# Both MLP products of a two-layer trunk in an order written by hand, with x fetched and turned beside the second product

## The chip, the cores and the metric

The kernel runs on one core of one Trainium2 chip. The metric is the device time of one execution in microseconds; less is better. A core has five engines that run their own instruction queues in order: TensorE (PE, the matmuls), VectorE (DVE), ScalarE (ACT), GpSimd (POOL) and SyncE (SP), which here issues nearly all DMA transfers. Engines meet through semaphores only. Data lives in SBUF (128 partitions), matmul results in PSUM (eight banks of 128 x 512 float32).

## The reference

The input is x, 1024 tokens x 1024 features, float32. Two layers follow, each a mixer and an MLP, and a last norm.

```python
for layer in range(DEPTH):
    h = rmsnorm(x, mix_norm_g[layer])
    x = x + (diff_attention(h, ...) if layer == 0 else recurrent_block(h, ...))
    x = x + sqrelu_mlp(rmsnorm(x, mlp_norm_g[layer]), mlp_w1[layer], mlp_w2[layer])
return rmsnorm(x, final_norm_g)

def sqrelu_mlp(h, w1, w2):          # w1: 1024 x 4096, w2: 4096 x 1024
    return jnp.square(jax.nn.relu(h @ w1)) @ w2
```

Only the two MLPs, `h @ w1` (the first product) and `relu(..)^2 @ w2` (the second), are touched by the change.

## The kernel before

**Numbers in two halves.** Each float32 operand is split into a high part (rounded by a ScalarE copy to fp32r) and a low part (operand minus high part, by VectorE; `split`, L83). A product then takes three matmuls: high x high, high x low, low x high.

**Seven products for eight.** Both MLP products are 2 x 2 block products computed with seven block products, by sums and differences of blocks (Winograd's form). The operands' sums are made on VectorE before they are split; the seven results are added up on the way out of PSUM. The norm's factor of a token is not applied to the first product's input: since relu squared is homogeneous, the second product's result is multiplied by `inv` = 1/(mean square + eps) (L895), spread over partitions for layer 0 (`spread`, L277), as a column per token block in layer 1.

**First product.** `parts_block` (L239) turns each block of x into the split block operands `self.sx[k]`, k = 0 to 3 (28 tiles of 128 x 1024), as the mixer's last product finishes, and stores x to DRAM (`xD`). The 32 blocks of 128 columns of `w1` are taken as 16 pairs, i and i+16. For each pair, `pair_weights` (L770) loads two blocks, makes the sums `s12` and `s34` and splits everything; `hidden_pair` (L794) does seven products of 12 matmuls (k = 0 to 3, three each; L809 to L811), adds them up in `ct` and `cl` (L814), applies relu and the square on ScalarE (L835, L836), makes the second product's sums (`h12`, `h34`, L840) and writes seven pieces of 128 x 512 to DRAM (`hid`, L843). In layer 1, pairs 3 to 10 each also turn one 128 x 1024 block of x (`turn_x`, L867): load from `xD`, eight transposes on TensorE (L874), a ScalarE copy (L876), a store to `xN`. After pair 1 the token's mean squares are summed on TensorE (L894).

**The planner.** Outside a `manual_schedule` block, the framework's planner orders the instructions of an engine by its own costs, and may put instructions of one pair ahead of another's. Inside such a block, the listed engines take the block's instructions in the order written; other instructions may still be put between them. Before, the first products are the planner's; the second products (L903) are in the written order on PE, ACT, DVE and SP.

**Second product.** `second` (L906) works through 56 slots of 24 matmuls (L1007 to L1009): 8 of kind P, 16 A, 16 B, 8 C and 8 D. P gives the first of the seven products, in banks `u` (two PSUM tiles of two banks each); A two at once, on `z` (four tiles of a bank) and further on `u`; B two, on `z` and `u`; C one on `z`; D one on `u`. A slot's operands are loaded four slots ahead (`load`, L931; at most four in the rings R and W) and made and split one slot ahead (`prepare`, L963). D of the last four slots is done one output block at a time. When a product is complete, `after` (L1069) empties its banks, and the rest of the adding goes into a list `side`, of which two or three steps run per slot (L1113). `x` itself is fetched in halves (`xr`, L1014) during B and added there. Where an output half is finished, `x_done` runs: in layer 0 the recurrence's norm and split (`norm_part`, L215), in layer 1 the final norm (`final_part`, L1135), which goes from ScalarE (squares) to VectorE to GpSimd (rsqrt) and back.

**Buffers.** Most tiles of 128 x 1024 float32 come from one ring, T, of 46; raw weights from R (4), some high parts and loaded hidden blocks from W (4).

Of the kernel before, what the change touches and what calls it, by code (L numbers as in the profile page):

```python
# [30 lines left out]
def rope_tables():  # L31

    inv = np.float32(1.0) / np.power(10000.0, np.arange(0, HD, 2) / HD).astype(np.float32)
    ang = np.arange(S, dtype=np.float32)[:, None] * inv[None, :]
    cos = np.cos(ang.astype(np.float64)).astype(np.float32).T
    sin = np.sin(ang.astype(np.float64)).astype(np.float32).T
    c = np.concatenate([cos, cos, cos, cos], axis=0)
    s = np.concatenate([-sin, sin, -sin, sin], axis=0)
    return np.ascontiguousarray(c), np.ascontiguousarray(s)


class Trunk:
# [727 lines left out]
    def pair_weights(self, w1, i):  # L770

        nc = self.nc
        top, low = (self.raw(w1[:, c : c + P].rearrange("(k p) m -> p k m", p=P), (P, NK, P)) for c in (i * P, DFF // 2 + i * P))
        a, b = slice(0, 4), slice(4, 8)
        s12, s34 = self.t4("s12", F32, (P, NK, P)), self.t4("s34", F32, (P, NK, P))
        sub = lambda out, x, y, op=ALU.subtract: nc.vector.tensor_tensor(out=out, in0=x, in1=y, op=op)  # L779
        sub(s12[:, a], low[:, a], low[:, b], ALU.add)  # L780
        sub(s12[:, b], s12[:, a], top[:, a])
        sub(s34[:, a], top[:, a], low[:, a])
        sub(s34[:, b], top[:, b], s12[:, b])
        th, tl = self.split(top, (P, NK, P), "wt", hi_tag="W")
        lw = self.t4("wl", F32R, (P, 2, 4, P))
        nc.scalar.activation(out=lw[:, 0], in_=low[:, b], func=AF.Copy)
        nc.vector.tensor_tensor(out=lw[:, 1], in0=low[:, b], in1=lw[:, 0].bitcast(F32), op=ALU.subtract)
        h12, l12 = self.split(s12, (P, NK, P), "ws", hi_tag="W")
        h34, l34 = self.split(s34, (P, NK, P), "ws")
        return {"A11": (th[:, a], tl[:, a]), "A12": (th[:, b], tl[:, b]), "A22": (lw[:, 0], lw[:, 1]),  # L790
                "S1": (h12[:, a], l12[:, a]), "S2": (h12[:, b], l12[:, b]),
                "S3": (h34[:, a], l34[:, a]), "S4": (h34[:, b], l34[:, b])}

    def hidden_pair(self, w, i, last):  # L794
# [6 lines left out]
        mm = nc.tensor.matmul  # L801
        p1, p2, p4 = self.acc1(), self.accg(), self.accg()
        p67, p53 = self.acc2(), self.acc2()
        l, r = slice(0, CH), slice(CH, S)

        def product(a, b, bank):
            for k in range(4):
                (ah, al), (bh, bl) = w[a], self.sx[k][b]
                mm(bank, ah[:, k], bh, start=k == 0, stop=False)  # L809
                mm(bank, ah[:, k], bl, start=False, stop=False)  # L810
                mm(bank, al[:, k], bh, start=False, stop=k == 3)  # L811

        def add(out, x, y, op=ALU.add):
            nc.vector.tensor_tensor(out=out, in0=x, in1=y, op=op)  # L814

        top, low = self.t4("ct"), self.t4("cl")
        product("A11", "B11", p1)
        nc.scalar.activation(out=top[:, l], in_=p1, func=AF.Copy)
        product("S2", "T2", p67[:, l])
        add(low[:, l], top[:, l], p67[:, l])  # L820
        product("S1", "T1", p53[:, l])
        add(low[:, r], low[:, l], p53[:, l])
        product("S4", "B22", p53[:, r])
        add(top[:, r], low[:, r], p53[:, r])
        product("S3", "T3", p67[:, r])
        both = low.rearrange("p (h c) -> p h c", c=CH)
        add(both, both, p67[:, None, r].to_broadcast([P, 2, CH]))
        product("A12", "B21", p2)
        add(top[:, l], top[:, l], p2)
        product("A22", "T4", p4)  # L830
        add(low[:, l], low[:, l], p4, ALU.subtract)


        for c in (top, low):
            nc.scalar.activation(out=c, in_=c, func=AF.Relu)  # L835
            nc.scalar.activation(out=c, in_=c, func=AF.Square)  # L836
        a12, a34 = self.t4("h12", F32, (P, 2, CH)), self.t4("h34", F32, (P, 2, CH))
# [4 lines left out]
        f = self.hid[i]  # L842
        put = lambda at, src: nc.sync.dma_start(out=f[:, at], in_=src)  # L843
        put(0, top[:, l])
        put(5, low[:, l])
        if last:
            two(a12[:, 0], top[:, r], low[:, r], ALU.add)
            two(a12[:, 1], a12[:, 0], top[:, l])
            two(a34[:, 0], top[:, l], top[:, r])
            two(a34[:, 1], low[:, l], a12[:, 1])  # L850
            put(3, a34[:, 1])
            put(6, low[:, r])
        else:
            two(a12[:, 0], top[:, r], top[:, l])
            two(a12[:, 1], low[:, r], a12[:, 0])
            two(a34[:, 0], low[:, r], top[:, r])
            two(a34[:, 1], low[:, l], a12[:, 1])
            put(3, low[:, r])
            put(6, a34[:, 1])
        put(slice(1, 3), a12)  # L860
        put(4, a34[:, 0])

    def mlp_first(self, layer):

        self.w = self.pair_weights(self.ins["mlp_w1"][layer], 0)

    def turn_x(self, m):  # L867

        nc = self.nc
        t = self.t4("xm")  # L870
        nc.sync.dma_start(out=t, in_=self.xD[m])
        ps = self.acc2()
        for k in range(NT):
            nc.tensor.transpose(ps[:, k * P : (k + 1) * P], t[:, k * P : (k + 1) * P], self.ident)  # L874
        kept = self.t4("xk", F32, (P, NT, P))
        nc.scalar.activation(out=kept, in_=ps.rearrange("p (k c) -> p k c", c=P), func=AF.Copy)  # L876
        nc.sync.dma_start(out=self.xN.rearrange("(t p) c -> p t c", p=P)[:, :, m * P : (m + 1) * P], in_=kept)

    def mlp(self, layer, last):

        nc = self.nc
        w1, w2 = self.ins["mlp_w1"][layer], self.ins["mlp_w2"][layer]
        ssacc = self.ssacc
        self.hid = [self.dram.tile([P, 7, CH], F32, name=f"hid{layer}_{b}") for b in range(16)]
        if last:
            self.xN = self.dram.tile([S, D], F32, name="xN")
        for i in range(16):
            now = self.w
            if i + 1 < 16:
                self.w = self.pair_weights(w1, i + 1)  # L890
            if i == 2:
                ps = self.acc1()
                for j in range(NT):
                    nc.tensor.matmul(ps[:, j : j + 1], ssacc[:, j * P : (j + 1) * P], self.ones, start=True, stop=True)  # L894
                inv = self.const.tile([P, NT], F32, name=f"inv{layer}")  # L895
                nc.vector.tensor_scalar(out=inv, in0=ps[:, :NT], scalar1=1.0 / D, scalar2=EPS, op0=ALU.mult, op1=ALU.add)
                nc.vector.reciprocal(out=inv, in_=inv)
            if i == 3 and not last:
                inv = self.spread(inv)
# [485 lines left out]
```

## Time and profile before

| | |
|---|---|
| Time, median of 3 runs | 2564.32 us (2564.13 to 2568.66) |
| Profiled execution: its time, its span | 2565.54 us, 2563.3 us |
| Mean granted TensorE clock | 0.938 |
| Busy: PE, DVE, ACT, POOL | 87%, 62%, 41%, 6% of the span |
| Layer 0: first product, second product | about 640 to 1033 us, 1040 to 1390 us |
| Layer 1: first product, second product | about 1725 to 2205 us, 2212 to 2556 us |

A line of a timeline gives start, duration, engine, line of the kernel, operation, tiles (out<-in) and a count; in brackets stands how long the engine was idle before it and what released it. A row by stretch gives its length, then for each engine the busy time and the number of instructions, then the mean granted TensorE clock, the share of time the DMA engines were busy, and their GB/s. A row of waits gives total, number of times, and longest. Matmul durations include the pipeline's depth, so what one costs is read from the distance between two starts. Tile names come from the program: `h2h` and `w2h` are high parts of the second product's operands, `wth`, `wsh` and `t12h` of the first's.

### The profile page before, as it was taken

How to read it: one execution, taken by the hardware profiler on the slowest of the kernel's cores; microseconds unless marked ns; L12 is line 12 of the kernel's file. 1: busy time of each engine (PE TensorE's matmuls, PEld its weight loads, DVE VectorE, ACT ScalarE, POOL GpSimd, SP SyncE). 2: the span in 40 equal slices, each digit the busy share in tenths (PEclk: the TensorE clock that was granted, in tenths of full speed). 3: DMA queues.
4: the chain of work that ended last, by engine and by line, in shares of the span. 5: the costliest groups of instructions: out<-in, count | busy, mean ns of one | idle time of the engine just before them, and what ended most of it. 6: DMA issues, size and time to landing. Idle time of an engine off the chain costs nothing.

```text
span 2563.3 us, 26499 instructions
## 1 busy us (share of the span) xinstructions
PE 2239.3 (87%) x9794; PEld 1799.7 (70%) x9794; DVE 1578.4 (62%) x2069; ACT 1059.8 (41%) x1616; POOL 163.1 (6%) x193
## 2 busy tenths in 40 slices
PE   8998799778789999899989989878866689899987
PEld 7777677666677777787668778666655567688775
DVE  5346677555866666496874777778443445666664
ACT  5235566544433333352343545544322223433343
POOL 3002111110400000000000000012000000000000
PEclk9999999889899999999989899998988889999997
DMA  6435446434243334685543011122433323756642
GB/s 190 117 77 140 117 108 166 114 111 156 74 136 119 132 126 151 229 289 211 202 148 107 25 41 45 46 82 81 129 123 118 120 97 117 284 201 217 230 148 99
DMA packets 241219, 347.44 MB, mean 136 GB/s; under 512 B 16097, under 2 KB 139074, under 8 KB 241090
## 3 DMA queue, kind: packets, MB, share of 16 engines
q1 hardware_dynamic: 232258, 318.48, 37.5%
q0 software_dynamic: 7680, 25.17, 4.3%
q10 hardware_dynamic: 1152, 2.10, 0.3%
q8 instruction: 77, 1.26, 0.2%
q14 instruction: 52, 0.43, 0.0%
HBM read 225.10 MB, written 87.03 MB: 122 GB/s over the span
## 4 chain that ended last, share of the span: by engine, by line
PE 35%; DVE 18%; ACT 11%; issue 6%; DMA 2%; SPq 0%; ACTq 0%; POOL 0%; DVEq 0%; POOLq 0%
PE acc L809 3%; PE acc L1009 3%; PE acc L1008 3%; PE acc L1007 3%; PE acc L811 3%; PE acc L810 3%; DVE s L779 3%; DMA xm<-x 2%; DVE wtl L92 1%; DVE h L840 1%; PE acc L333 1%; ACT cl L836 1%; ACT cl L835 1%; PE acb L1009 1%; PE acb L1008 1%
## 5 line engine op out<-in xcount | busy, mean ns | idle before, releaser
L92 DVE TENSOR_TENSOR h2l<-h,h2h 128x1024 fp32r<-128x1024 f32 x112 | 136.9, 1222 | 68.8 <-ACT h2h L89 68.1
L835 ACT ACTIVATE ct<-ct 128x1024 f32<-128x1024 f32 x32 | 33.9, 1060 | 321.9 <-DVE ct L814 321.9
L490 ACT ACTIVATE p<-acc,nmax 128x768 f32<-128x768 f32 (+7 forms) x128 | 95.4, 745 | 150.7 <-DVE nmax L507 58.5
L89 ACT ACTIVATE w2h<-w 128x1024 fp32r<-128x1024 f32 x80 | 84.1, 1052 | 136.8 <-DVE w L922 112.5
L814 DVE TENSOR_TENSOR ct<-cl,acc 128x512 f32<-128x512 f32 x32 | 22.0, 688 | 186.4 <-PE acc L811 186.4
L333 PE MATMUL acg<-xgh,wh 128*128 128x512 f32 x320 | 135.7, 424 | 0.0
L89 ACT ACTIVATE wsh<-s 128x1024 fp32r<-128x1024 f32 x64 | 67.2, 1051 | 153.4 <-DVE s L779 153.3
L165 POOL TENSOR_TENSOR rstd<-ms,mhalf 128x4 f32<-128x4 f32 (+2 forms) x25 | 25.0, 1000 | 1643.9 <-DVE ms L163 1623.2
L89 ACT ACTIVATE h2h<-h 128x1024 fp32r<-128x1024 f32 x112 | 117.3, 1047 | 29.4 <-DMA h<-hid 28.5
L336 PE MATMUL acg<-xgh,wl 128*128 128x512 f32 x320 | 127.9, 400 | 0.0
L334 PE MATMUL acg<-xgl,wh 128*128 128x512 f32 x320 | 127.7, 399 | 0.0
L92 DVE TENSOR_TENSOR w2l<-w,w2h 128x1024 fp32r<-128x1024 f32 x80 | 97.8, 1222 | 47.1 <-ACT w2h L89 47.1
L1007 PE MATMUL acc<-w2h,h2h 128*128 128x512 f32 x256 | 105.4, 412 | 19.9 <-ACT w2h L89 11.3
L1007 PE MATMUL acc<-h2h,w2h 128*128 128x512 f32 x256 | 101.5, 396 | 8.1 <-DVE h L840 6.9
L1008 PE MATMUL acc<-w2l,h2h 128*128 128x512 f32 x256 | 104.8, 409 | 4.3 <-DVE w2l L92 4.3
L809 PE MATMUL acc<-t12h,wsh 128*128 128x512 f32 x256 | 104.3, 410 | 0.1
L1009 PE MATMUL acc<-w2h,h2l 128*128 128x512 f32 x256 | 103.9, 406 | 0.0
L810 PE MATMUL acc<-t12l,wsh 128*128 128x512 f32 x256 | 103.4, 404 | 0.0
L1009 PE MATMUL acc<-h2h,w2l 128*128 128x512 f32 x256 | 101.7, 397 | 1.5 <-DVE w2l L92 1.5
L811 PE MATMUL acc<-t12h,wsl 128*128 128x512 f32 x256 | 102.9, 402 | 0.0
L1008 PE MATMUL acc<-h2l,w2h 128*128 128x512 f32 x256 | 101.5, 396 | 0.4 <-DVE h2l L92 0.4
L92 DVE TENSOR_TENSOR wsl<-s,wsh 128x1024 fp32r<-128x1024 f32 x64 | 78.3, 1225 | 25.8 <-ACT wsh L89 25.8
(362 smaller groups left out, 6365.6 us busy)
## 6 DMA issues: line engine op xcount, KB each, us to landing
w<-in_mlp_w_dram SPq DMA_DIRECT2D x96, 512.0 KB, 4.8
raw<-in_mlp_w_dram SPq DMA_DIRECT2D x64, 512.0 KB, 4.8
h<-hid SPq DMA_DIRECT2D x64, 512.0 KB, 5.3
h<-hid SPq DMA_DIRECT2D x96, 256.0 KB, 4.8
w<-in_mlp_w_dram SPq DMA_DIRECT2D x80, 256.0 KB, 3.8
hid<-cl SPq DMA_DIRECT2D x64, 256.0 KB, 2.1
hid<-h SPq DMA_DIRECT2D x32, 512.0 KB, 3.1
hid<-h SPq DMA_DIRECT2D x64, 256.0 KB, 4.2
```

Of the source, the lines that this page charges most:

```text
L89: nc.scalar.activation(out=hi, in_=src, func=AF.Copy)
L92: (lo_eng or nc.vector).tensor_tensor(out=lo, in0=src, in1=hi.bitcast(F32), op=ALU.subtract)
L333: mm(ps[:, pc], a, xh[:, cs], start=(k == 0), stop=False)
L334: mm(ps[:, pc], a, xl[:, cs], start=False, stop=False)
L336: mm(ps[:, pc], b, xh[:, cs], start=False, stop=(k == n - 1))
L490: nc.scalar.activation(out=p[c][:, :n], in_=src, func=AF.Exp, bias=nmax[:, c : c + 1], accum_out=sums[:, c : c + 1])
L809: mm(bank, ah[:, k], bh, start=k == 0, stop=False)
L810: mm(bank, ah[:, k], bl, start=False, stop=False)
L811: mm(bank, al[:, k], bh, start=False, stop=k == 3)
L1007: mm(bank[m], ah, bh, start=first, stop=False)
L1008: mm(bank[m], ah, bl, start=False, stop=False)
L1009: mm(bank[m], al, bh, start=False, stop=end)
```

## The change

`hidden_pair` and `turn_x` go; the loop over pairs moves into `mlp`, inside one `manual_schedule` block with the second product. A pair's work is now named steps (`th`, `s12`, `tl`, ... for the next pair's weights; `rt`, `st`, `rl`, `sl`, `t12`, `t34` for the pair before; `e6` its last add), and the loop writes which steps stand between which two products. Raw weights are loaded two pairs ahead. Pair 0's high parts come from ring T. The second product's first two slots are loaded, and slot 0 prepared, within pair 15.

The second product is a class, `Second`. Slots, kinds and rings are as before, but `prepare` runs two slots ahead, makes the sums ahead of the splits, and the additions are regrouped: x is loaded whole into the output tiles and scaled sums are added to it (in layer 0 one 512 KB load in each P slot). In layer 1 the eight blocks of x are loaded in slots 0 to 3, and slots 4 to 7 each turn two output tiles by sixteen transposes ahead of their products, emptied by ScalarE; `xN` is gone. Additions wait in a list with a cost each, and each kind of slot has a budget (`drain`). The final norm's gain is loaded at the start of layer 1's second product.

```diff
+    def prepare(self, s):
...
+        if kind == "A":
...
+            one = w[:, 0] if last else w[:, 1]
+            if last:
+                tt(one, w[:, 1], w[:, 0])
+                tt(k, side, one)
...
+        elif kind == "D" and last:
+            tt(w, w, self.kept[i // 2])
+        xh, xl = self.k.split(x, (P, 2, CH), "h2")
...
+    def complete(self, m, half, steps):
+        def fn():
+            for step in steps:
+                step()
+            self.k.x_done(m, half)
+        self.also(0.7 * (len(steps) + 2), fn)
...
+    def drain(self, budget=1e9):
+        self.credit = min(self.credit + budget, 1e9)
+        while self.side and self.credit >= self.side[0][0]:
+            cost, fn = self.side.pop(0)
+            self.credit -= cost
+            fn()
...
+    def turn_x(self, s):
+        if not self.last:
+            t = k.t4("x")
+            nc.sync.dma_start(out=t, in_=k.xD[s])
+            k.x.append(t)
+            return
+        if s < 4:
+            for m in (2 * s, 2 * s + 1):
+                self.xm.append(k.t4("xm"))
+                nc.sync.dma_start(out=self.xm[m], in_=k.xD[m])
+            return
+        for t in (2 * s - 8, 2 * s - 7):
+            x = k.t4("x")
+            k.x.append(x)
+            for h, ps in ((0, k.acc1()), (1, k.accg())):
+                for j in range(4):
+                    nc.tensor.transpose(ps[:, j * P : (j + 1) * P], self.xm[4 * h + j][:, t * P : (t + 1) * P], k.ident)
+                nc.scalar.activation(out=x[:, h * CH : (h + 1) * CH], in_=ps, func=AF.Copy)
...
+    def run(self):
...
+        if self.last:
+            k.final_begin()
+        N = len(self.slots)
+        budget = {"P": 0.0, "A": 1.4, "B": 1.45, "C": 2.9, "D": 2.9}
+        for s in range(AHEAD):
+            self.load(s)
+        self.prepare(0)
+        for s in range(N - TAIL_SLOTS):
+            self.load(s + AHEAD)
+            self.prepare(s + 1)
+            self.prepare(s + 2)
+            kind, pairs = self.slots[s]
+            if s < 8:
+                self.turn_x(s)
+            if s == 8:
+                self.z = [k.acc1(), k.acc1(), k.accg(), k.accg()]
+            for n in range(2):
+                self.products(s, n)
+                if pairs[n] == 15:
+                    self.after(kind, n)
+            del self.parts[s]
+            self.drain(budget[kind])
...
     def mlp(self, layer, last):
...
+                product("A11", "B11", p1)
+                if "e6" in before:
+                    before["e6"]()
+                do("th", "s12", "rt", "st")
+                product("S2", "T2", p67[:, l])
+                nc.scalar.activation(out=top[:, l], in_=p1, func=AF.Copy)
+                do("tl", "s34", "rl", "sl")
+                product("S1", "T1", p53[:, l])
+                add(low[:, l], top[:, l], p67[:, l])
+                do("h12", "lh", "t12", "l12")
+                product("S4", "B22", p53[:, r])
+                add(low[:, r], low[:, l], p53[:, l])
+                do("h34", "t34", "l34")
+                product("S3", "T3", p67[:, r])
+                add(top[:, r], low[:, r], p53[:, r])
+                do("ll")
+                product("A12", "B21", p2)
+                both = low.rearrange("p (h c) -> p h c", c=CH)
+                add(both, both, p67[:, None, r].to_broadcast([P, 2, CH]))
...
+                if i == 15:
+                    second.prepare(0)
+                product("A22", "T4", p4)
+                add(top[:, l], top[:, l], p2)
+                before = self.hidden_steps(i, top, low, last)
+                before["e6"] = lambda low=low, p4=p4: add(low[:, l], low[:, l], p4, ALU.subtract)
+            for name in ("rt", "st", "e6", "rl", "sl", "t12", "t34"):
+                before[name]()
+            self.sx = None
+            second.run()
```

In a step's name, `th`, `h12`, `h34`, `lh` are ScalarE copies to the high part; `tl`, `l12`, `l34`, `ll` VectorE's low parts; `s12` and `s34` two VectorE operations each on halves; `rt` and `st` relu and square of `top` on ScalarE, `rl` and `sl` of `low`; `t12` and `t34` two VectorE operations each, followed by writes to `hid`. `do` runs the named steps of the next pair's weights and of the pair before.

More of the change, by code (lines that the diff above doesn't have):

```diff
@@ L767, in out_group, with pair_raws, pair_weights @@
             next(beside, lambda: None)()
[L770 removed]
+    def pair_raws(self, w1, i):
+        return [self.raw(w1[:, c : c + P].rearrange("(k p) m -> p k m", p=P), (P, NK, P)) for c in (i * P, DFF // 2 + i * P)]
+    def pair_weights(self, raws, i):
         nc = self.nc
[L776 removed]
+        top, low = raws
         a, b = slice(0, 4), slice(4, 8)
[L778 to L792, printed above, removed]
@@ L800, in hidden_pair, with mlp_first, mlp @@
+    def mlp_first(self, layer):
+        w1 = self.ins["mlp_w1"][layer]
+        steps, self.w = self.pair_weights(self.pair_raws(w1, 0), 0)
+        for name in ("th", "s12", "tl", "s34", "h12", "lh", "l12", "h34", "ll", "l34"):
+            steps[name]()
+    def mlp(self, layer, last):
         nc = self.nc
         mm = nc.tensor.matmul
-        p1, p2, p4 = self.acc1(), self.accg(), self.accg()
-        p67, p53 = self.acc2(), self.acc2()
+        w1, w2 = self.ins["mlp_w1"][layer], self.ins["mlp_w2"][layer]
+        self.hid = [self.dram.tile([P, 7, CH], F32, name=f"hid{layer}_{b}") for b in range(16)]
@@ L804, in hidden_pair, with means @@
         l, r = slice(0, CH), slice(CH, S)
[L806 to L811, printed above, removed]
+        box = {}
+        def means():
+            ps = self.acc1()
+            for j in range(NT):
+                nc.tensor.matmul(ps[:, j : j + 1], self.ssacc[:, j * P : (j + 1) * P], self.ones, start=True, stop=True)
+            inv = self.const.tile([P, NT], F32, name=f"inv{layer}")
+            nc.vector.tensor_scalar(out=inv, in0=ps[:, :NT], scalar1=1.0 / D, scalar2=EPS, op0=ALU.mult, op1=ALU.add)
+            nc.vector.reciprocal(out=inv, in_=inv)
+            box["inv"] = inv
+            self.ssacc = None
@@ L839, in two @@
-        def two(out, x, y, op=ALU.subtract):
-            nc.vector.tensor_tensor(out=out, in0=x, in1=y, op=op)
[L842 to L859, printed above, removed]
@@ L879, in mlp @@
[L879 to L899, printed above, removed]
-            if last and 3 <= i < 3 + NK:
-                self.turn_x(i - 3)
-            self.hidden_pair(now, i, last)
-        with self.tc.manual_schedule(engines={EPE, EACT, EDVE, ESP}):
-            self.second(w2, inv, last)
```

497 lines of the change are left out of this document (266 added, 231 removed).

## The prediction

> **What bounds the kernel now.** I read the page's busy times first, then the table of busy time by stretch, cut at the ends of the four MLP stages, and then the waits and the timeline inside each stretch.
>
> ```profile
> PE 2239.3 (87%) x9794; PEld 1799.7 (70%) x9794; DVE 1578.4 (62%) x2069; ACT 1059.8 (41%) x1616; POOL 163.1 (6%) x193
> ```
> ```profile
> core 0: us, PE busy (x) PEld busy (x) DVE busy (x) ACT busy (x) POOL busy (x), PEclk, DMA share, GB/s
> 689.30:1032.60 343.30, 317.44 (x1327) 253.38 (x1327) 211.44 (x279) 123.50 (x139) 0.00 (x0) 0.96 0.40 133
> 1032.60:1389.90 357.30, 331.33 (x1391) 263.52 (x1391) 247.89 (x303) 143.33 (x172) 0.00 (x0) 0.97 0.58 203
> 1762.20:2205.40 443.20, 345.96 (x1375) 272.60 (x1375) 209.82 (x278) 130.29 (x144) 0.00 (x0) 0.88 0.37 122
> 2205.40:2563.30 357.90, 322.58 (x1345) 258.89 (x1344) 225.51 (x275) 140.44 (x180) 4.42 (x8) 0.94 0.56 193
> 880.00:901.14 21.14, 19.63 (x85) 15.61 (x85) 13.75 (x19) 8.09 (x9) 0.00 (x0) 1.00 0.42 137
> 2135.90:2157.03 21.13, 19.62 (x85) 15.62 (x84) 13.56 (x19) 8.09 (x10) 0.00 (x0) 1.00 0.43 138
> 1938.70:1972.83 34.13, 23.47 (x94) 18.35 (x93) 13.74 (x19) 9.11 (x10) 0.00 (x0) 0.85 0.36 116
> 1843.90:1848.50 4.60, 4.51 (x15) 3.93 (x16) 0.00 (x0) 1.51 (x2) 0.00 (x0) 0.50 0.10 30
> 2230.00:2240.00 10.00, 10.00 (x46) 8.29 (x45) 7.01 (x8) 4.31 (x5) 0.00 (x0) 1.00 1.03 405
> 2240.00:2260.00 20.00, 20.00 (x90) 16.57 (x89) 0.00 (x0) 0.00 (x0) 0.00 (x0) 1.00 0.25 97
> ```
> ```profile
> 1149.75 0.39 PE L1007 MATMUL acc<-h2h,w2h 128*128 128x512 f32 x1
> ...
> 1155.19 0.39 PE L1007 MATMUL acc<-h2h,w2h 128*128 128x512 f32 x1
> ```
>
> TensorE is the bound, with holes. The last two rows stand 24 matmuls apart: 5.44/24 = 0.2267 us a matmul. Each product of each MLP is 16 pairs x 84 = 56 slots x 24 = 1344 matmuls, so 304.6 us at full pace. The four stretches take 343.3, 357.3, 443.2 and 357.9 us (the first and third begin after some matmuls are done, below). VectorE has room: 13.75 us of a pair's 21.14.
>
> The largest hole is in layer 1's first product. A pair takes 21.13 us (2135.9), but 34.13 (1938.7) when a block of x is turned in it:
>
> ```profile
> PE acc L874 <- DMA xm<-x: 54.6, 8, 7.5
> ```
>
> This row of TensorE's waits after 1780 us says why: the transposes stand in its queue ahead of products that are ready, waiting for x, and afterwards the granted clock is 0.50 (the stretch at 1843.9), which doubles a matmul: these 4.6 us lose 2.3.
>
> The smaller hole is in every pair: 84 x 0.2267 = 19.04, so 2.1 us of 21.14 is lost.
>
> ```profile
> 879.97 0.50 PE L809 MATMUL acb<-b,wth 128*128 128x512 f32 x1 [0.87 <-ACT ct L818]
> ...
> 881.35 0.50 PE L809 MATMUL acc<-t34h,wsh 128*128 128x512 f32 x1 [0.64 <-DVE cl L814]
> ```
>
> A product into `p67`'s right half waits for an add that reads its left half: the tile is guarded as one.
>
> **First products by hand: steady state.** No arithmetic is added; the order changes. With the start of A11 at 0 and 2.72 us a product, A22 ends at 19.04. I follow VectorE with the durations of these rows:
>
> ```profile
> L92 DVE TENSOR_TENSOR wsl<-s,wsh 128x1024 fp32r<-128x1024 f32 x30 | 36.7, 1226 | 16.0 <-ACT wsh L89 16.0
> L814 DVE TENSOR_TENSOR cl<-ct,acc 128x512 f32<-128x512 f32 x16 | 10.9, 681 | 4.3 <-ACT ct L818 4.3
> ...
> L835 ACT ACTIVATE ct<-ct 128x1024 f32<-128x1024 f32 x16 | 17.0, 1062 | 140.8 <-DVE ct L814 140.8
> ```
>
> `e6` to 1.0, `s12` 2.3, `tl` 3.6, `s34` 4.9, first add (S2 ends 5.4) 6.4, `t12` 7.8, `l12` 9.0, second add (it reads `p53`, so counted behind S4's 10.9) 11.8, `t34` 13.2, `l34` 14.4, third 15.1, `ll` 15.8, the double add 17.0, last 17.7. ScalarE has eight operations of about 1.06 and two halves, under 10 us. All parts of the next pair are ready by 16, its banks by 17.7: no product waits, and each read stands one product behind its write, so no bank guard bites. I take 19.04 a pair; the ends are 19.04 and today's 21.14.
>
> SyncE too is ordered: the next loads, two pairs ahead, stand before the seven writes to `hid` that wait for `sl`, `t12` and `t34`. Behind them only loads needed 19 us later wait. Tiles of the big ring are the risk. At 8 us into a pair live 28 of `sx`, the spread `inv`, two `tl`, `s12`, `s34`, two `l12`, two `wl`, four of `h34` and `l34`, two each of `ct` and `cl`, and `h12`: 46 of 46.
>
> **The starts of the first products.** All k of A11 now come first, and k=3 needs the last `sx`; before, products of k=0 to 2 were mixed in.
>
> ```profile
> 688.63 0.68 DVE L269 TENSOR_TENSOR b<-z,b 128x512 fp32r<-128x512 f32 x1
> ```
> ```profile
> 1759.33 2.83 DVE L269 TENSOR_TENSOR b<-z,b 128x512 fp32r<-128x512 f32 x1
> ```
> ```profile
> 699.38 1.95 PE L894 MATMUL acb<-ones,ssacc 128*128 128x1 f32 x16 [2.11 <-ACT ct L818]
> ```
>
> This low half of the last `b11` ends at 689.3 in layer 0 and 1762.2 in layer 1, with only nine matmuls done by then: 1335 x 0.2267 = 302.6, the sixteen small products of L894 2, in layer 0 eight of the spread 1, and 4 for the half clock after the wait (0 to 7; the stretch at 1843.9 lost 2.3, and this wait is longer). Layer 0: 310 for 343.3, gain 33. Layer 1, with `turn_x` gone: 308.6 for 443.2, gain 134.6.
>
> **The second products.** Before, they open with a hole and lose time where evictions are bunched:
>
> ```profile
> 1039.60 0.80 PE L1007 MATMUL acc<-h2h,w2h 128*128 128x512 f32 x1 [6.88 <-DVE h L840]
> ```
> ```profile
> 1279.23 0.39 PE L1009 MATMUL acg<-h2h,w2l 128*128 128x512 f32 x1
> 1286.44 0.79 PE L1007 MATMUL acb<-h2h,w2h 128*128 128x512 f32 x1 [6.83 <-ACT w2h L89]
> ```
>
> After: slot 0 is prepared inside the last pair, so the 6.9 goes. Slot 1 is prepared behind that pair's tail: `e6`, `rl`, `sl`, `t12`, `t34`, two splits, 8.1 us after the last product against slot 0's 5.4: 2.7 late and 2.3 of half clock, 5 (0 to 11: today 6.9, and 4 more in slot 0). The writes to `hid` now stand on SyncE ahead of loads 2 and 3, so slot 2 is ready at about 16.5, and slot 1 ends at 15.7: within the same 5.
>
> The arithmetic in the middle is moved, not changed: by count 76 half-tile operations on VectorE in layer 0 before and after, 44 in layer 1. Gone are the sixteen `xr` reads, and in layer 1 the eight writes to `xN`; new are eight loads of x of 512 KB beside the P slots. In layer 0 a P slot so moves 1.5 MB, 3.9 us at the 405 GB/s of the stretch at 2230, under its 5.44, and nobody waits for x before slot 8; I cost it at nothing. If that cover goes (1.5 MB at the 203 GB/s that the whole stretch has is 7.7 us), it is 8 x 2.3 = 18.
>
> Preparing two slots ahead gives 10.9 us of cover. In layer 0 a B slot costs VectorE two halves, two splits (3.8) and a budget of 1.45: 5.27 under 5.44. The eight scalings after B are 8 x 0.68 = 5.4, begun when the first bank closes 2 us ahead: 3.4 behind B's last product, then 2.4 of preparing: under 10.9. I take 2 us late in all (0 to 15). The stretch also holds 1391-1344 = 47 matmuls of the recurrence, 10.7. Layer 0: 304.6+10.7+5+2 = 322.3 for 357.3, gain 35.
>
> Layer 1 gets the turning of x. Sixty-four transposes, by this row of eight (their tail is 0.2 of it) 0.11 each, cost 7.2:
>
> ```profile
> 576.51 1.06 PE L533 MATMUL acb<-ident,p 128*128 128x128 f32 x8
> ```
>
> Those of slot 4 need all eight blocks of x. Behind the last pair's writes (1.75 MB from 3.3 us after its last product) SyncE sends `gb` 0.5, slots 2 to 7 6, x 4: 12.25 MB, at the 405 GB/s of the fullest stretch 31.7 us. A write of 256 KB lands in 2.0 or 4.2 us, of which 0.6 is its moving, so 1.4 is added:
>
> ```profile
> hid<-h SPq DMA_DIRECT2D x64, 256.0 KB, 4.2
> ...
> hid<-ct SPq DMA_DIRECT2D x32, 256.0 KB, 2.0
> ```
>
> x is there at 3.3+31.7+1.4 = 36.4; TensorE is at slot 4 at 21.8+5 = 26.8. It waits 9.6 us, then loses 2.3 at half clock: 12 (0 if loads run ahead, 16 if SyncE waits for a ring slot). Their evictions, four of 0.6 a slot on ScalarE, stand behind the preparing of two slots more and have 5.4 us.
>
> The Trainium skill (DMA: Bandwidth & Descriptors, Specifications) puts HBM to one core at about 358 GB/s. By that estimate x lands 4 us later and the sum is 4 us longer; the row's 405 over 10 us does not agree, so I keep the row.
>
> At the end, the outputs' norms block VectorE:
>
> ```profile
> 2485.97 0.68 DVE L1145 TENSOR_TENSOR fy<-x,gb 128x512 f32<-128x512 f32 x1
> ...
> 2490.54 0.48 DVE L1152 TENSOR_SCALAR fy<-fy,rstd 128x512 f32<-128x512 f32 x1 [0.67 <-POOL rstd L165]
> ```
> ```profile
> 2505.45 1.22 DVE L922 TENSOR_TENSOR w<-w,s 128x1024 f32<-128x1024 f32 x1
> ...
> 2510.13 1.22 DVE L922 TENSOR_TENSOR w<-w,s 128x1024 f32<-128x1024 f32 x1
> ```
>
> Two norms take 5 us; a D slot takes 4.7 today because its difference stands behind x's split. Ahead of it, it is three operations back to back, 3.4. With slots 48 and 49 prepared at the end of slot 47, slots 50 to 55 are ready 9.5, 17.9, 21.3, 24.7, 28.1 and 31.6 us later, so the last tail slot ends near 33 instead of 27.2, plus waits on the shared bank tile: 9 late (0 to 27).
>
> ```profile
> 2555.77 0.39 PE L1009 MATMUL acc<-w2h,h2l 128*128 128x512 f32 x1
> ```
>
> From here to the end 7.5 us stay. Sum: 304.6+7.2+5+12+9+7.5 = 345.3 for 357.9, gain 12.6.
>
> **Sum.** 33+134.6+35+12.6 = 215. The profiled execution took 2565.5 (span 2563.3 and 2.2 around it), 1.2 above the median shown: 2350.5 on its scale, about 2350 on the median's. Attention and recurrence are taken as unchanged.
>
> **Rivals.**
> 1. The second products gain nothing: the side work bunches elsewhere. For it: VectorE is within 0.2 us of the slot in B. Against: `2240.00:2260.00` shows VectorE and ScalarE idle, so far ahead do they run. 2350+35+12.6 = 2398. Chance 0.13.
> 2. Pairs stay at 21.14, from waits between engines that my order of 16 us misses: 32 x 2.1 = 67, so 2417. Chance 0.10.
> 3. Transposes don't hold the clock up. The clock would fall beside each sixteen, as at 1843.9 (2.3 lost), in slots 4 to 7: 9.2, so 2359. Against: the eight at 576.51 ran at full pace between other work. Chance 0.07. The Trainium skill (TensorE: Matmul & The Clock Gate, Part 4: PE-mode transpose) says that transposes do not count as busy for the clock; no row here shows sixteen in a row at full clock.
> 4. Slower: the ring of 46 is one tile short in the hand order. ScalarE, in order, would then hold the eviction of A11 until `ct` of the pair before is free, after `e6`, `rl`, `sl`, `t12`, `t34` and a landing of 4.2: some 9.3 after the pair's end, 6.6 after A11. With 2.3 of half clock 8.9 x 32 = 285: 2635. It decides from 215/32 = 6.7 us a pair. Against: the count fits. Chance 0.05.
> 5. The change only moves the wait for x: the eight loads queue behind slots' loads and TensorE waits in slot 4 for all that it waits today, 8 x (34.13-21.13) = 104 us in place of 12: 2442. Against: 12.25 MB take 32 us. Chance 0.03.
>
> **Numbers.** The forecast has 0.62; its own range is 2330 to 2372, the ends of the start, x and norm terms. The range 2318 to 2405 adds rivals 1 and 3, and below it the case that all of 5+2+12+9 vanish. Faster: all but rival 4, 0.93; slower 0.05; same 0.02. About 0.2%, 5 us, is what a measurement can tell from no change.
>
> **What would show it.** Pairs of 19.0 in both layers, no line of `xm` among waits of the first product; the second's first matmul within 0.5 us of the last product; one wait for `xm` or a transpose of some 9 us near slot 4; slots of 5.44 through B and C; a wait of a few us near the end. Pairs over 20, or D slots over 7, would make it wrong.

## The result, and the profile after

| | before | after |
|---|---|---|
| Time, median (range) | 2565.57 us (2564.13 to 2568.66) | 2326.66 us (2326.02 to 2327.85) |
| Profiled execution: its time, its span | 2565.54 us, 2563.3 us | 2326.84 us, 2325.1 us |
| Mean granted TensorE clock | 0.938 | 0.968 |

The ratio is 0.907 (95% interval 0.905 to 0.908): 238.7 us less on the profiled executions, where the sum of the prediction had 215. Busy times of the page after; TensorE is now at work for 92% of the span, with the same 9794 matmuls:

```profile
PE 2146.2 (92%) x9794; PEld 1760.4 (76%) x9794; DVE 1569.5 (68%) x2069; ACT 1064.1 (46%) x1624; POOL 161.6 (7%) x193
```

The table by stretch after, cut where the one before was cut: at the end of the low half of each layer's last `b11`, and at the ends of the products.

```profile
core 0: us, PE busy (x) PEld busy (x) DVE busy (x) ACT busy (x) POOL busy (x), PEclk, DMA share, GB/s
673.20:982.40 309.20, 309.12 (x1367) 256.18 (x1368) 211.59 (x283) 128.53 (x143) 0.00 (x0) 0.99 0.42 141
982.40:1310.00 327.60, 319.93 (x1401) 262.13 (x1400) 240.35 (x299) 139.90 (x169) 0.00 (x0) 1.00 0.65 227
1310.00:1670.40 360.40, 314.72 (x1332) 252.45 (x1330) 275.45 (x238) 180.68 (x178) 31.14 (x12) 0.94 0.16 53
1670.40:1977.50 307.10, 307.02 (x1350) 254.19 (x1351) 211.53 (x283) 126.92 (x139) 0.00 (x0) 0.99 0.43 142
1977.50:2325.10 347.60, 321.19 (x1409) 262.50 (x1407) 217.88 (x271) 145.66 (x193) 4.40 (x8) 0.97 0.59 207
770.00:789.04 19.04, 19.04 (x86) 15.77 (x85) 13.49 (x19) 8.22 (x9) 0.00 (x0) 1.00 0.46 151
1900.00:1919.04 19.04, 19.04 (x85) 15.77 (x84) 13.49 (x18) 8.22 (x10) 0.00 (x0) 1.00 0.47 153
```

In the last two rows a pair takes 19.04 us and TensorE is busy for all of it. The first cut is at this row's end, the fourth cut at the other's:

```profile
672.54 0.68 DVE L518 TENSOR_TENSOR b<-z,b 128x512 fp32r<-128x512 f32 x1
```
```profile
1667.59 2.83 DVE L518 TENSOR_TENSOR b<-z,b 128x512 fp32r<-128x512 f32 x1
```

Before, these ended at 689.3 and 1762.2. Stretch by stretch, with the rows of before that the prediction shows:

| Stretch | before | after | gain | predicted gain |
|---|---|---|---|---|
| up to layer 0's last `b11` | 689.3 | 673.2 | 16.1 | 0 |
| layer 0, first product | 343.3 | 309.2 | 34.1 | 33 |
| layer 0, second product | 357.3 | 327.6 | 29.7 | 35 |
| recurrence, up to layer 1's last `b11` | 372.3 | 360.4 | 11.9 | 0 |
| layer 1, first product | 443.2 | 307.1 | 136.1 | 134.6 |
| layer 1, second product | 357.9 | 347.6 | 10.3 | 12.6 |

The four products gave 210.2 of the 215 predicted; 28 more came from two stretches that were taken as unchanged. The waits of TensorE in layer 1's second product after:

```profile
PE acg L246 <- DMA xm<-x: 8.5, 4, 3.5
PE acc L144 <- DVE w2l L341: 5.4, 5, 2.2
PE acc L143 <- ACT w2h L338: 3.5, 3, 1.5
```

The first row is slot 4's transposes waiting for x, in four pieces; from slot 3's first matmul to slot 4's, 10.5 us were lost beyond the slot and the sixteen transposes.

### The profile page after: what moved, and what is told of

It is laid out like the page before. It is cut to its first block, busy times and chain, and to the rows that moved or that the text cites. A ratio compares the mean times of both kernels' runs of the same rounds, so it can differ in the third digit from the quotient of the medians.

```text
span 2325.1 us, 26433 instructions
## 1 busy us (share of the span) xinstructions
PE 2146.2 (92%) x9794; PEld 1760.4 (76%) x9794; DVE 1569.5 (68%) x2069; ACT 1064.1 (46%) x1624; POOL 161.6 (7%) x193
## 4 chain that ended last, share of the span: by engine, by line
PE 53%; DVE 10%; ACT 5%; DMA 2%; issue 2%; SPq 0%; POOL 0%; ACTq 0%; POOLq 0%; DVEq 0%
PE acc L1184 5%; PE acc L1185 5%; PE acc L1186 5%; PE acc L145 4%; PE acc L143 4%; PE acc L144 4%; PE acg L1184 2%; PE acg L1186 2%; PE acg L1185 2%; PE acb L145 2%; PE acb L144 2%; PE acb L143 2%; PE acg L145 2%; PE acg L144 2%; PE acg L143 2%
## 5 line engine op out<-in xcount | busy, mean ns | idle before, releaser
L1086 ACT ACTIVATE ct<-ct 128x1024 f32<-128x1024 f32 x64 | 68.0, 1063 | 263.8 <-DVE ct L1155 262.8
L338 ACT ACTIVATE h2h<-h 128x1024 fp32r<-128x1024 f32 x112 | 117.7, 1050 | 55.3 <-DMA h<-hid 44.9
L1155 DVE TENSOR_TENSOR cl<-cl,acc 128x512 f32<-128x512 f32 x64 | 61.0, 953 | 75.2 <-PE acc L1186 75.2
L1184 PE MATMUL acc<-t12h,w12h 128*128 128x512 f32 x256 | 101.6, 397 | 0.0
L1185 PE MATMUL acc<-t12l,w12h 128*128 128x512 f32 x256 | 101.5, 396 | 0.0
L1186 PE MATMUL acc<-t12h,w12l 128*128 128x512 f32 x256 | 101.3, 396 | 0.0
L792 PEld LDWEIGHTS acb<-v,aT 128*128 128x128 f32 x576 | 73.6, 195 | 30.1 <-ACT aT L959 24.8
L792 PE MATMUL acb<-v,aT 128*128 128x128 f32 x576 | 78.9, 283 | 14.4 <-ACT aT L959 13.6
```

The costliest lines, as they stand in the source:

```text
L338: nc.scalar.activation(out=hi, in_=src, func=AF.Copy)
L792: nc.tensor.matmul(ps[:, :P], aT[:, j * P : (j + 1) * P], v[j // 2][:, j % 2, e], start=(j == 0), stop=(j == i))
```

## The experiments

Times are medians; the kernel before, run beside them, took 2563.9 to 2565.8 us. "Less" and "more" for an edit of the kernel after are against 2326.7, for one of the kernel before against the runs of before beside it.

**1 and 2. Why the first products begin earlier.** The part of the diff that touches the stretches ahead of them is the ring of pair 0's high parts. One kernel puts it back, the other gives it to the kernel before.

```diff
-            "th": lambda: high("wt", lambda: top, full, "W" if i else "T"),
+            "th": lambda: high("wt", lambda: top, full, "W"),
...
-            "h12": lambda: high("w12", lambda: t["s12"], full, "W" if i else "T"),
+            "h12": lambda: high("w12", lambda: t["s12"], full, "W"),
```

> The kernel after, with the high parts of pair 0's weights taken from the small ring W, as in the kernel before. In question: why layer 0's first product could begin 16 us earlier than my sum had it (last low half of b11 at 673.2 instead of 689.3), and layer 1's 12 us earlier. Theory 1, the written order keeps the first product's matmuls out of the mixer's last product, so that its blocks and the parts made from them come sooner: the ring does not matter, the time stays 2327 (2323 to 2331). Rival, ring W: pair 0's high parts no longer take two of the four places that the mixer's own weights need; then putting them back costs what was gained, 12 to 28 us: 2339 to 2355.

```diff
-        th, tl = self.split(top, (P, NK, P), "wt", hi_tag="W")
+        th, tl = self.split(top, (P, NK, P), "wt", hi_tag="W" if i else "T")
...
-        h12, l12 = self.split(s12, (P, NK, P), "ws", hi_tag="W")
+        h12, l12 = self.split(s12, (P, NK, P), "ws", hi_tag="W" if i else "T")
```

> The kernel before, with the high parts of pair 0's weights taken from the big ring T, as in the kernel after; the same question from the other side. Theory 1 (order): the time stays 2565.5 (2561 to 2570). Rival (ring W): 12 to 28 us less, 2538 to 2553.

Measured: after with ring W 2350.7 us, 24.0 more; before with ring T 2537.6, 27.6 less (four runs, 2534.2 to 2545.2). The rival held on both sides, my first theory fell. The four high parts of the mixer's last weights (`woh`), by tile, first in the kernel after, then with ring W; the row gives durations, the first and the last start:

```profile
L338 ACT ACTIVATE woh<-raw x4: 1058/1064/1065, 606.2 to 630.1; 128x1024 fp32r<-128x1024 f32 x4
...
  PE acc L582: 0.8, 1
```
```profile
L338 ACT ACTIVATE woh<-raw x4: 1041/1042/1057, 613.5 to 660.8; 128x1024 fp32r<-128x1024 f32 x4
...
  PE acc L582: 6.9, 3
```

Each of these weights takes two of ring W's four places (its high and its low part), and pair 0's `wth` and `w12h` hold the other two until the first product is done with them. So the mixer's weights are split one at a time, each after the blocks before it: the last at 660.8 instead of 630.1, and TensorE waits for them three times, 6.9 us. With ring W the last `b11` is there 15.5 us later:

```profile
688.02 0.68 DVE L518 TENSOR_TENSOR b<-z,b 128x512 fp32r<-128x512 f32 x1
```

In layer 1 the stretch from the end of layer 0's second product to the last `b11` is 8.9 us longer with ring W. Together that is 24.4 of the 28.0 us; the rest was not followed.

**3. How much of the turning of x is a late load.** The load goes one pair ahead of its transposes.

```diff
+    def load_x(self, m):
+        self.xm = self.t4("xm")
+        self.nc.sync.dma_start(out=self.xm, in_=self.xD[m])
...
             if last and 3 <= i < 3 + NK:
                 self.turn_x(i - 3)
+            if last and 2 <= i < 2 + NK:
+                self.load_x(i - 2)
```

> The kernel before, with each load of a block of x issued one pair ahead of the pair in which it is turned; nothing else moves. Theory: the 104 us that I gave to turning x in layer 1's first product, 8 pairs x (34.13 - 21.13), are a load issued too late with products queued behind the transposes, and not the work of the transposes (8 x 0.9 us): with the load a pair ahead (21 us) against waits of 8 to 55 us most of it goes: 2460 to 2490. Rival, the load queues behind the weights on SyncE or for a place in the ring, whenever it is issued: at most 20 us go, 2545 to 2566; then the gain of the change came from where the turning went and not from when x was asked for.

Measured: 2493.3 us, 71.9 less, 3 us above what was expected. Waits of TensorE in layer 1's first product, where the kernel before had `xm` at 54.6:

```profile
PE acc L809 <- ACT xk L880: 25.2, 8, 3.2
PE acc L809 <- DVE cl L814: 5.9, 11, 1.5
```
```profile
1896.70:1923.70 27.00, 22.59 (x94) 17.51 (x92) 13.74 (x18) 9.00 (x10) 0.00 (x0) 0.94 0.45 146
```

A pair with turning takes 27.0 instead of 34.1. The wait for x is gone, and a smaller one has come in its place: a product into a tile of two banks, which the transposes hold until ScalarE has copied it out. About two thirds of the 104 us were the load's lateness; whether other banks would save the rest was not run.

**4. What the second slot of cover is worth.** In the kernel after the line goes that prepares two slots ahead.

```diff
             self.prepare(s + 1)
-            self.prepare(s + 2)
```

> The kernel after, with each slot of the second products prepared one slot ahead, as before, instead of two. Theory: the second slot of cover (10.9 us instead of 5.4) is what keeps the eight scalings behind B and the output's norms from stopping TensorE; without it layer 0 waits some 4 us at the first C slots and some 5 before the tail, layer 1 some 5 at the end, each with 2.3 of half clock behind it: 2327 + 15 to 25, so 2342 to 2352, and slots 40 to 43 and 50 to 55 are the ones that grow. Rival, the order of the side work by budgets does it alone: 2325 to 2332.

Measured: 2337.9 us, 11.3 more, below what I expected. Layer 0's second product is 2.5 us longer, layer 1's 8.3, mostly in slots 48 to 53. Waits in the latter, to be read beside 3.5 and 5.4 of the kernel after:

```profile
PE acc L143 <- ACT w2h L337: 6.4, 4, 3.1
PE acc L144 <- DVE w2l L340: 6.0, 6, 2.2
```

The place is right and the size was too large: the second slot of cover is worth about half of what I gave it, and only about 2 us of it lie behind B in layer 0.

**5. The planner orders the first products of the kernel after.** Only the second products stay in the written order.

```diff
-        with self.tc.manual_schedule(engines={EPE, EACT, EDVE, ESP}):
+        with ExitStack():
             second = self.second(w2, box, last)
...
-            second.run()
+            with self.tc.manual_schedule(engines={EPE, EACT, EDVE, ESP}):
+                second.run()
```

> The kernel after, with the planner ordering the first products again (the second products stay in the written order); program text, rings and the place of x's turning are those of after. Theory: the 2.1 us that each pair lost were the planner's order on VectorE, ScalarE and TensorE, so pairs go back to about 21.1: 32 x 2.1 = 67 more, and perhaps some us at the starts: 2380 to 2410. Rival, the place of the adds in the program (each one product behind its bank) is what saves the 2.1 and the planner keeps it: pairs of 19.0 to 19.5, 2325 to 2345.

Measured: 2307.8 us (2303.3 to 2309.8), 18.9 less than the kernel after. That is below even my rival's 2325 to 2345. The pairs under the planner, and pair 0 under it; then pair 0 of the kernel after:

```profile
654.00:684.20 30.20, 23.53 (x86) 17.49 (x85) 30.06 (x26) 16.74 (x19) 15.83 (x6) 0.83 0.12 43
770.00:789.04 19.04, 19.04 (x86) 15.77 (x85) 13.31 (x19) 8.21 (x9) 0.00 (x0) 1.00 0.48 153
1900.00:1919.04 19.04, 19.04 (x85) 15.77 (x85) 13.30 (x19) 8.21 (x9) 0.00 (x0) 1.00 0.45 153
```
```profile
652.10:693.10 41.00, 24.14 (x85) 18.09 (x84) 34.24 (x30) 18.66 (x21) 15.73 (x6) 0.71 0.16 54
```

Given the new program text, the planner makes the same 19.04 us a pair, and in pair 0 it does better: it takes products of k = 0 to 2 while k = 3 is missing, where the written order lets TensorE wait inside A11 at every k. Pair 0 is 10.8 us shorter in layer 0 and, at 37.8 for 46.5, 8.7 in layer 1: about the 18.9. TensorE under the planner: products of S2 (`t12h`, `w12h`) and A22 (`t34h`, `wl`) run ahead of A11's last k:

```profile
655.33 0.39 PE L1184 MATMUL acc<-t12h,w12h 128*128 128x512 f32 x1
...
671.38 0.39 PE L1184 MATMUL acg<-t34h,wl 128*128 128x512 f32 x1
...
675.27 0.50 PE L1185 MATMUL acb<-b,wth 128*128 128x512 f32 x1 [1.44 <-DVE b L518]
```

The waits of TensorE from 600 to 700 us in the kernel after are nearly all for `b11` (`b`):

```profile
PE acb L1185 <- DVE b L518: 12.2, 2, 6.7
PE acb L1184 <- ACT b L517: 4.7, 2, 2.6
```

**6 and 7. What made a pair 21.1.** In the kernel after the first three adds go back to where they stood before, right behind the products they read; in the kernel before they go one product later.

```diff
                 product("S1", "T1", p53[:, l])
-                add(low[:, l], top[:, l], p67[:, l])
+                add(low[:, r], low[:, l], p53[:, l])
                 do("h12", "lh", "t12", "l12")
                 product("S4", "B22", p53[:, r])
-                add(low[:, r], low[:, l], p53[:, l])
+                add(top[:, r], low[:, r], p53[:, r])
```

(and the first of the three behind S2.)

> The kernel after, written order kept, but the first three adds of a pair stand right behind the product whose bank they read, as in the kernel before. S4, into the right half of p53, must then wait for the add that reads the left half: S1's end to the add's end is about 0.2 + 0.68 us. Theory: the guard on the whole tile is about half of the 2.1 us lost in a pair: pairs of 19.9 to 20.3, so 32 x 0.9 to 1.2: 2354 to 2368. Rival, in the written order VectorE reaches these adds only later, behind other operations, and holds S4 longer: 2 us or more a pair, 2390 or more. If the guard costs nothing: 2325 to 2332.

```diff
         product("S2", "T2", p67[:, l])
-        add(low[:, l], top[:, l], p67[:, l])
         product("S1", "T1", p53[:, l])
-        add(low[:, r], low[:, l], p53[:, l])
+        add(low[:, l], top[:, l], p67[:, l])
         product("S4", "B22", p53[:, r])
-        add(top[:, r], low[:, r], p53[:, r])
+        add(low[:, r], low[:, l], p53[:, l])
         product("S3", "T3", p67[:, r])
+        add(top[:, r], low[:, r], p53[:, r])
```

> The kernel before, planner and all, with one edit in a pair of the first products: the first three adds stand one product later in the program, where the kernel after has them. Theory, formed from the two runs before (the planner with after's program makes pairs of 19.04; the written order with adds right behind makes 20.47): the 2.1 us that a pair lost were the place of the adds in the program, through the guard on p67 and p53, and no hand order was needed. Then pairs outside x's turning fall from 21.1 to 22.6 to about 19.0 to 19.3, layer 0 gains some 37 us over its 15 pairs, layer 1 some 29: 2495 to 2520. Rival, the planner needs after's other rewriting as well (loads of weights two pairs ahead, a pair's tail written beside the next pair's products): 2545 to 2566.

Measured: 2373.1 us, 46.5 more than the kernel after, 5 above what the theory gave; and 2470.8, 93.2 less than the kernel before. The end of S1 and the start of S4 in the first of the two, then VectorE between them:

```profile
848.22 0.39 PE L1186 MATMUL acc<-t12h,w12l 128*128 128x512 f32 x1
849.75 0.47 PE L1184 MATMUL acc<-b2h,w34h 128*128 128x512 f32 x1 [1.15 <-DVE cl L1155]
```
```profile
848.33 0.69 DVE L1035 TENSOR_TENSOR s<-raw,s 128x512 f32<-128x512 f32 x1
848.93 0.68 DVE L1155 TENSOR_TENSOR cl<-cl,acc 128x512 f32<-128x512 f32 x1
```

S4 starts 1.53 us after the start of S1's last matmul instead of 0.23, and plain pairs come to 20.47: 32 x 1.43 = 46. Of the 1.53 the add takes 0.68 and the way from its end to S4 0.14. The 0.71 ahead of it hold the matmul itself and also the difference that VectorE still has in hand, so the expectation's rival, VectorE reaching the add late, has a part in it; how large a part was not taken apart.

The kernel before with the three lines moved, a plain pair and one with x turned in it, and TensorE's wait in its layer 1's first product from pair 3 on for the landing of x; then two rows of the kernel before from the same pairs:

```profile
770.00:789.04 19.04, 19.04 (x86) 15.77 (x85) 13.67 (x19) 8.33 (x10) 0.00 (x0) 1.00 0.47 153
1857.80:1888.70 30.90, 21.72 (x94) 17.60 (x92) 13.73 (x18) 9.23 (x10) 0.00 (x0) 0.89 0.40 127
```
```profile
PE acc L874 <- DMA xm<-x: 54.9, 8, 7.4
```
```profile
PE acg L809 <- DVE cl L814: 14.5, 7, 2.1
PE acb L809 <- ACT ct L818: 5.8, 5, 2.5
```

With nothing in the first products written by hand, plain pairs take 19.04, and the waits for `cl` and `ct` that the kernel before had are gone in these pairs: the only other row there is for `wtl`, 16.5 us, which had 15.2 before. It is more than I expected: the pairs with turning are shorter too (30.9 for 34.1), and so is pair 0, by 4.1 us in layer 0 and 5.9 in layer 1.

**8. The three small edits of the kernel before together** (experiments 2, 3 and 7).

> The kernel before, planner and all, with the three small edits of the earlier runs together: the first three adds of a pair one product later (alone 93 us), pair 0's high parts in the big ring (alone 27.6), each block of x loaded one pair ahead of its turning (alone 71.9). Theory: the three are separate holes of TensorE, so the gains add: 2564 - 192 = 2372, 2360 to 2385; and what is then left to the kernel after, some 45 us, are its second products (the trace gives them 29.7 us in layer 0 and 10.3 in layer 1). Rival, the holes cover each other (x's turning has less cover when pairs are shorter, the big ring has no place for both edits): 2390 or more, and the hand order of after was worth more than its second products.

Measured: 2382.8 us, 183.0 less than before: 95% of the 192 that they give one by one. What is left to the kernel after is 56 us. Its rows:

```profile
973.90:1329.40 355.50, 331.28 (x1391) 263.43 (x1391) 245.42 (x300) 141.35 (x170) 0.00 (x0) 0.97 0.58 203
2025.40:2381.10 355.70, 322.31 (x1345) 258.74 (x1344) 223.53 (x273) 138.41 (x178) 4.43 (x8) 0.95 0.56 194
1787.60:1811.40 23.80, 21.90 (x94) 17.68 (x93) 13.73 (x18) 9.11 (x10) 0.00 (x0) 0.93 0.51 166
```

The second products of the kernel after are 27.9 and 8.1 shorter; it saves the turning, 8 x (23.80 - 19.04) = 38; and it loses 18.9 to the planner (experiment 5): 55.

**9. The wait for x in layer 1's second product.**

```diff
-        if self.last:
-            k.final_begin()
...
-            if s < 8:
+            if s < (4 if self.last else 8):
                 self.turn_x(s)
+            if s == 8 and self.last:
+                k.final_begin()
...
                 self.products(s, n)
+                if n == 1 and self.last and 5 <= s < 8:
+                    self.turn_x(s)
...
-        for t in (2 * s - 8, 2 * s - 7):
+        for t in {5: (0, 1, 2), 6: (3, 4, 5), 7: (6, 7)}[s]:
```

> The kernel after, in layer 1's second product only: the blocks of x are turned behind the products of slots 5, 6 and 7 (3, 3 and 2 of them) instead of ahead of those of slots 4 to 7, and gb is loaded at slot 8 instead of ahead of everything. Theory: the 10.4 us for which slot 4's transposes wait are x's landing behind 12.25 MB; x lands at about the same time, 1.3 us earlier without gb, while TensorE comes to the transposes two slots (10.9 us) later: the wait and its half clock go, 2327 - 9 to 13, so 2314 to 2318. Rival, the wait is for something else that moves along (a bank of PSUM, a ring slot for the turned x): 2325 or more.

Measured: 2313.6 us, 13.1 less. No row of TensorE's waits in this product names `xm` any more; its two largest:

```profile
PE acc L144 <- DVE w2l L343: 5.1, 5, 2.2
PE acc L143 <- ACT w2h L340: 2.0, 2, 1.2
```

Slot by slot, 11.6 us of the gain are the wait for x and the half clock behind it. Some 2 more lie at slots 1 and 2, which lose 5.2 us instead of 7.1; `gb` no longer stands ahead of the loads there, but it was not moved by itself.

**10. VectorE beside GpSimd.**

```diff
-            nc.gpsimd.tensor_tensor(out=self.ssacc, in0=self.ssacc, in1=sq, op=ALU.add)
+            nc.vector.tensor_tensor(out=self.ssacc, in0=self.ssacc, in1=sq, op=ALU.add)
...
-        h2, l2 = self.split(d, (P, S), "b2", lo_eng=nc.gpsimd)
+        h2, l2 = self.split(d, (P, S), "b2")
```

> The kernel after, with GpSimd's share of the parts of x (the sum of squares and the low part of b2) done by VectorE. In question: the 2.8 us that some 128x512 differences take on VectorE while GpSimd works, instead of 0.68. Theory 1, they get in each other's way: between the mixer's last product and the start of the first product in earnest six such differences of layer 0 (652 to 673) go back to 0.68, 11.7 us less, and VectorE takes over six operations of 1.22, 7.3 more: 4 us; layer 1 5: together 2315 to 2320. Theory 2, the long durations are a wait for data inside the operation, which stays: VectorE only gets 7 us more work at each start: 2335 to 2342.

Measured: 2309.6 us, 17.1 less, twice what I expected. One group of differences (two tiles from SBUF, 128x512) in the stretch ahead of layer 0's first product; the columns are busy time and mean ns of one. In the kernel after, then without GpSimd:

```profile
L511 DVE TENSOR_TENSOR t<-z,t 128x512 f32<-128x512 f32 x4 | 6.9, 1716 | 0.2
```
```profile
L511 DVE TENSOR_TENSOR t<-z,t 128x512 f32<-128x512 f32 x4 | 2.7, 685 | 0.6 <-ACT z L497 0.6
```

All of VectorE's 128x512 differences in the two starts go back to 0.68 or 0.69. Theory 1 holds. I had counted only the differences between the mixer's last product (652) and the last `b11`; slow operations stand ahead of it too, such as this one, with 1.22 in most of its group:

```profile
638.50 2.98 DVE L341 TENSOR_TENSOR t34l<-t,t34h 128x1024 fp32r<-128x1024 f32 x1
```

**11 and 12. Together.** First experiments 5, 9 and 10 in one kernel; then with `b11` and the first half of `t12` made as soon as blocks 0 to 3 are there:

> The kernel after with three edits of the earlier runs together: the planner orders the first products, x is turned behind slots 5 to 7, and VectorE does GpSimd's share of the parts of x. Each alone gave 18.9, 13.1 and 17.1 us. x's turning lies elsewhere than the others and adds in full; the planner and VectorE's share both shorten the starts of the first products. If the two are the same idle time: 2326.7 - 18.9 - 13.1 = 2295. If they add up: 2278. I expect 2280 to 2290, part shared.

```diff
+        if k < 4:
+            b11 = self.t4("b11", F32R, (P, 2, CH))
+            nc.scalar.activation(out=b11[:, 0], in_=b[:, l], func=AF.Copy)
+            nc.vector.tensor_tensor(out=b11[:, 1], in0=b[:, l], in1=b11[:, 0].bitcast(F32), op=ALU.subtract)
+            t12 = self.t4("t12")
+            sub(t12[:, l], b[:, r], b[:, l])
+            self.early[i] = b11, t12
         if b is None or d is None:
             return
...
+        b11, t12 = self.early.pop(i)
```

> The same three edits, and b11 and the first half of t12 are made as soon as the block of x that they need is there, instead of with the block four later. Theory: after the mixer's last product TensorE waits for the low half of the last b11 behind VectorE's work for the last blocks; b11 needs only blocks 0 to 3, so the first product A11 can run at once, and the wait left is that for the last t12: 5 to 12 us less than without this edit: 2270 to 2285. Rival, what holds the start is the sum of VectorE's work in these 20 to 30 us, in whatever order: within 3 us of the run without it.

Measured: 2271.3 us, then 2264.5 (2263.1 to 2266.4), both below their ranges; the step between them, 6.8, lies in the 5 to 12 that the theory gave. The three give 55.3 together, more than the 49.1 one by one. Part of the extra lies at slots 1 and 2 of layer 1's second product, which lose 2.4 us with all three and 5.2 to 8.8 with one of them; why they help one another there was not taken apart. The last kernel is at 0.883 of the kernel before (0.882 to 0.885) and 62 us under the one that the change made. Its busy times, and pair 0 of each layer:

```profile
PE 2134.6 (94%) x9794; PEld 1755.7 (78%) x9794; DVE 1546.9 (68%) x2091; ACT 1060.7 (47%) x1624; POOL 102.5 (5%) x171
```
```profile
650.60:669.60 19.00, 19.00 (x85) 15.76 (x84) 18.95 (x25) 9.71 (x11) 0.00 (x0) 1.00 0.12 39
1617.10:1643.10 26.00, 22.62 (x85) 16.23 (x84) 25.74 (x31) 15.24 (x18) 0.00 (x0) 0.93 0.06 24
```

In layer 0 pair 0 runs at full pace; in layer 1 VectorE is busy for 25.74 of 26.00 us and sets it.

## Why the prediction was right, and where it was not

The time of 2326.7 lies in the range of 2318 to 2405, 3 us below the forecast's own range of 2330 to 2372. The sum was 24 us short: two stretches gave 28 that it did not have, the four products 5 less than it had.

- **"Attention and recurrence are taken as unchanged"** is the step that failed. Pair 0's high parts come from another ring; the text ahead of the prediction says so, and the sum has no price for it. I followed ring T into the pairs and not ring W into the mixer's last product, its user just before. Experiments 1 and 2 give 24.0 and 27.6 for it.
- **First products, 19.04 a pair**: right. **Starts**: 310 predicted, 309.2; 308.6 predicted, 307.1 (two terms were a little off: the spread is sixteen matmuls, 1.8 us, not eight and 1; the half clock cost about 3, not 4). But the reason was half wrong. "By hand" was not needed: the place of the adds was the cause, and three lines of program text remove the 2.1 us (experiment 7). The prediction read the guard on the tile rightly from the wait at 881.35; how the wait for `ct` ahead of it hangs on the adds was not taken apart. The hand order, in pair 0, costs 18.9 us against the planner. "All k of A11 now come first" was counted as a fact of the change, not as a loss that it makes.
- **Layer 1's turning of x**: right, from the row of `xm`. Experiment 3 splits the 104 us: 72 are a load asked for too late.
- **Layer 0's second product**: 327.6 for 322.3. No hole at its start, as foreseen; slots 1 and 2 lose 4.1 and 1.2 against 5. The terms that were too small: "2 us late in all" was about 5, all near the tail (slots 51 and 52), and some 55 of the recurrence's matmuls, 12.5 us, fell into this stretch instead of 47, 10.7.
- **Layer 1's second product**: 347.6 for 345.3. The transposes cost 7.2 of 7.2, x 10.5 us of waiting against 9.6, with half clock 11.6 against 12; slots 50 to 54 lost 9.5 against 9; the tail took 7.4 against 7.5. The start was 7.1 against 5. The wait came out near its forecast because both sides were late: x about 39 us after the last product instead of 36.4, TensorE at the transposes at about 29 instead of 26.8.
- **The range.** Its lower end stood for the case that the terms 5, 2, 12 and 9 vanish. They measured 5.3, about 5, 11.6 and 9.5; what brought the time down to 2326.7 was the term that the sum did not have. That it lies inside the range is in part luck.
- **Rivals.** 1 (nothing from the second products) and 2 (pairs of 21.14) fell by the table by stretch. 4 (one tile short) and 5 (the wait for x only moved) fell with the pairs of 19.04 and the `xm` row of 8.5. 3 fell too:

```profile
2032.20:2034.30 2.10, 2.10 (x20) 1.97 (x19) 0.55 (x1) 1.08 (x3) 0.00 (x0) 1.00 0.93 314
2034.30:2039.30 5.00, 5.00 (x24) 4.10 (x23) 3.04 (x4) 2.97 (x6) 0.00 (x0) 1.00 0.47 135
```

Sixteen transposes in a row (the first stretch) and the slot behind them ran at a granted clock of 1.00, and slots with them took 1.8 us more, 16 x 0.11; right behind the wait for x, at a clock of 0.50, a transpose took 0.21. The rule of the Trainium skill on which that rival leaned (TensorE: Matmul & The Clock Gate, Part 4: PE-mode transpose) does not show here, where the transposes stand between dense products.

- **The rate of transfers.** The wait for x ended in this stretch:

```profile
2006.00:2020.00 14.00, 5.46 (x22) 4.12 (x21) 3.59 (x4) 4.63 (x7) 0.00 (x0) 0.67 1.04 402
```

402 GB/s over 14 us agrees with the 405 that the sum used. The 358 that the Trainium skill has for one core, half of a stack's 716 (DMA: Bandwidth & Descriptors, Specifications), is passed, with one core at work.

## What to carry to other kernels

When a kernel under a planner loses a fixed time in every round, look first at where in the program an add reads one half of a tile whose other half the next product writes: one product of distance was worth 93 us here, with no hand order in these products. When tiles change their ring, price it at every user of both rings, ahead of the stage that changes as well as in it. An order written by hand holds where operands arrive early; where they arrive one by one, a strict order waits for each, and the planner's mixing was worth 18.9 us.

## What the hardware showed that I had not expected

A 128x512 operation of VectorE with both inputs in SBUF that begins while GpSimd works takes up to 2.9 us instead of 0.68, and one with an input in PSUM (`acg`) does not. VectorE in the kernel after, then GpSimd at the same time:

```profile
660.21 0.67 DVE L996 TENSOR_TENSOR x<-x,acg 128x512 f32<-128x512 f32 x1
...
669.80 2.82 DVE L511 TENSOR_TENSOR t<-z,t 128x512 f32<-128x512 f32 x1
```
```profile
659.70 2.79 POOL L341 TENSOR_TENSOR b2l<-z,b2h 128x1024 fp32r<-128x1024 f32 x1
...
669.29 2.79 POOL L341 TENSOR_TENSOR b2l<-z,b2h 128x1024 fp32r<-128x1024 f32 x1
```

The first row lies inside GpSimd's first operation and takes 0.67. The second begins inside the second one, which ends at 672.08, and ends 0.54 after it: as if it waited until GpSimd was done and then took about its own time. At the two starts of the kernel after, all 19 such operations that begin inside one of GpSimd's end 0.55 or 0.56 us after it. In the kernel before, two at 1746 us took 0.68 even so, and there GpSimd's own operation took 3.72, its longest of these. This is what the Trainium skill says (SBUF — State Buffer, Who interferes with whom): a VectorE instruction with two SBUF inputs contends with a GpSimd instruction that reads SBUF, one with at most one, outside VectorE's two-port modes, does not. The help of GpSimd at the two starts cost VectorE more than it took off it: without it the kernel is 17.1 us faster (experiment 10).
